# Stick-breaking attention: both heads of a pair in one step, scores on the two row halves in turn, values as float32 products into one bank

## The chip, the cores and the metric

The kernel runs on one core of one Trainium2 chip. The metric is the device time of one execution in microseconds (us); the time of the kernel before is the median of three runs. Engines carry the names of the profile: PE is TensorE (matmuls), PEld its weight loads, DVE VectorE, ACT ScalarE, POOL GpSimd, SP SyncE, whose queue issues the DMAs.

## The reference, cut to what matters

Two layers. Each projects the normalised rows (512 and 16 meta rows, 1,024 wide) into three mixers: stick-breaking attention (6 heads of 64), retention (6 heads of 64) and an S5 state-space mixer (256 wide). Their outputs go through one output projection, and an MLP follows. The part that is changed:

```python
def stick_breaking(q, k, v):
    for blk in range(L // CHUNK):
        z = jnp.einsum('bhqd,bhkd->bhqk', qb, kb).astype(jnp.float32) * scale
        mask = (s_idx[None, :] < t_idx[:, None]) & (s_idx[None, :] >= PAD_FRONT)
        log1m = jnp.where(mask, jax.nn.log_sigmoid(-z), 0.0)
        between = lax.cumsum(log1m, axis=3, reverse=True) - log1m
        w = jnp.where(mask, jnp.exp(jax.nn.log_sigmoid(z) + between), 0.0)
        outs.append(jnp.einsum('bhqk,bhkd->bhqd', w.astype(vb.dtype), vb))
    return jnp.concatenate(outs, axis=2)
```

## The kernel before, in words

Activations lie transposed: 128 channels on the partitions, 528 rows (16 meta rows and 512) along the free axis. A pair of 64-channel heads fills one tile of 128 partitions, so there are three pairs of stick-breaking heads, three pairs of retention heads, and two tiles of S5. Most weights and activations are split into a rounded part (`hi`, `wh`, `xh`) and a rest (`lo`, `wl`, `xl`), and `mm3` makes three products of them for each 128 x 128 block of weights.

**One order for everything, made while the program is built.** `mm3` emits the large projections one matmul after another, and after each step `tick` lets up to `TICKS` waiting tasks go on. A task is a generator (one attention group, one retention pair, the S5 lane, a norm of heads); it emits a few instructions and gives way. It goes on when a modelled clock of the engines (`busy`, fed by `spend`) has reached its time and its condition holds. The engines run what was emitted in that order. Two counters limit the tasks: `free["bank"]`, 5 of the 8 PSUM banks (`BANKS`), from which a task takes banks and to which it gives them back, and `free["group"]` (`GROUPS`, 7), the score groups in flight.

**Score groups.** The lower triangle of a head's 528 x 528 scores is cut into three groups of columns, each in one bank `z`: A (pieces of 272, 144 and 16 columns), B2 (256, 144, 16) and B1 (256, 256). `sb_group` (L815) takes one bank, adds the mask as a bfloat16 product with the identity where the group has one, and adds the score products `z<-sq,sk`, float32, with a contraction of 64: one head lies on one half of the partitions. ACT and DVE then make softplus, POOL and ACT split it, triangular and ones matrices sum it on PE into the same bank (`z<-hi,tri`, `z<-hi,ones`), ACT takes the exponential `e`, and `slow_split` cuts `e` into `hi` (ACT) and `lo` (POOL).

**Values.** `sb_head` (L856) runs one head: group A, then B2 and B1. The values stand as [hi | lo] side by side in 128 columns (`vparts`, L894), and `av` gathers `v x hi` and `v x lo` of `e` over 128 partitions; ACT copies the lower half (`avl`), DVE adds it to the upper half (`sbo`), and when both heads of a pair are done, `slow_split` cuts `sbo` for the output projection (`mix[p]`). Two lanes, `sb_lane(0)` and `sb_lane(1)` (L1083), each go through the three pairs by themselves.

**The rest of a layer.** `ret_lane` runs the three retention pairs (`rtp` transposes, `kv`, `sc`, `ro`, `hps`), `s5_lane` the S5 mixer: a scan, `yps` matmuls, eight `ysm` operations for each of two halves, a gelu on `y`, then `s5_glu` (L789), two `mm3` of `hi`/`lo` of `ysm` with the weights `wglu` (rows `pj<-hi,hi`, `pj<-lo,hi`, `pj<-hi,lo`), a sigmoid and a product. All take banks from the same five. The output projection of a layer comes in three parts: `OUT_PARTS[0]` is (0,1,2), (6,7), (3,4,5), where 0 to 2 are the stick-breaking pairs, 3 to 5 the retention pairs and 6 and 7 S5. Ahead of each part `drain` lets tasks go on, without any projection between them, until the part's inputs have been emitted. In layer 1 the order is (6,7), (0,1,2), (3,4,5).

Nearly all operations of DVE, ACT and POOL carry the line of the helper `issue` (L121), all matmuls but transposes L132, transposes L138.

Of the kernel before, what the change touches and what calls it, by code (L numbers as in the profile page):

```python
# [15 lines left out]
P = 128  # L16
# [5 lines left out]
DFF = 2816  # L22
NF = DFF // P
HALF = T // 2
NT_SLOTS = 60
AHEAD = 4
WLAG = 1000
LEAD = 200
# [1 line left out]
DMA = 3500  # L30
TICKS = 6
BANKS = 5
GROUPS = 7
HOLD = (2, 0)
WENG = (1, 1, 0)
EPS = 1e-6
# [52 lines left out]
def hybrid_kernel(ctx, tc, A, out, dbg=None):  # L89
# [70 lines left out]
    def bank(s="b"):  # L160
        return mx.tile([P, 512], F32, tag="mx", name=nm(s))
# [16 lines left out]
    def banks(n):  # L178
        yield from take("bank", n)
# [676 lines left out]
    def sb_head(q, k, v, hh, o):  # L856

        r = slice(64 * hh, 64 * hh + 64)
        def weights(groups):
            hl, ws = {}, {}  # L860
# [7 lines left out]
        yield from take("group", len(sets[0]))  # L868
        started.append(weights(sets[0]))
        for groups in sets:  # L870
            ws = started[-1]
            if groups is sets[0]:
                yield from take("group", len(sets[1]))
                started.append(weights(sets[1]))
            yield lambda: len(ws) == len(groups)
# [8 lines left out]
            ws.clear()  # L884
            yield
            freed(len(groups), "group")
# [7 lines left out]
    def vparts(vt):  # L894

        v = vp.tile([P, 1280], F32R, tag="v", name=nm("v"))
        v4 = v.rearrange("p (j h c) -> p j h c", h=2, c=P)
        for j0, nj in ((0, 4), (4, 1)):
            yield from banks(1)
            ps = bank("vps")  # L900
            for j in range(nj):
                TE.transpose(ps[:, P * j:P * j + P], vt[:, KT0[j0 + j]:KT0[j0 + j] + P], ident)
            yield
            pv = ps[:, :P * nj].rearrange("p (j h d) -> p j h d", h=2, d=64)
            for hh in range(2):
                SC.copy(out=v4[:, j0:j0 + nj, hh, 0:64], in_=pv[:, :, hh, :])
            yield
            for hh in range(2):
                V.tensor_tensor(out=v4[:, j0:j0 + nj, hh, 64:128], in0=pv[:, :, hh, :],
                                in1=v4[:, j0:j0 + nj, hh, 0:64].bitcast(F32), op=ALU.subtract)  # L910
            yield
            freed(1)
        return v4


    def rotate(t, p, which):
# [137 lines left out]
    for l in range(LAYERS):  # L1054
# [15 lines left out]
        def after(n, p, t, l=l, got=got):  # L1070

            yield
            if n in ("sq", "sk"):
# [2 lines left out]
                yield from headnorm(t, (94 if n == "rq" else 96) + l)  # L1076
                t = yield from rotate(t, p, 0 if n == "rq" else 1)
            elif n == "sv":
                yield lambda: p < 2 or (("done", p - 2, 0) in got and ("done", p - 2, 1) in got)
                t = yield from vparts(t)  # L1080
            got[n, p] = t

        def sb_lane(hh, l=l, got=got, mix=mix):  # L1083
            for p in range(3):
                yield lambda: all((n, p) in got for n in ("sq", "sk", "sv"))
                if ("sbo", p) not in got:
                    got["sbo", p] = tt("sbo")
                yield from sb_head(got["sq", p], got["sk", p], got["sv", p], hh, got["sbo", p])
                got["done", p, hh] = True
                if ("done", p, 1 - hh) in got:  # L1090
                    dump(f"sb{l}{p}", got["sbo", p])
                    mix[p] = yield from slow_split(got["sbo", p])

        def ret_lane(l=l, got=got, mix=mix):
            for p in range(3):
# [12 lines left out]
                mix[6 + i] = yield from slow_split(so[i])  # L1108

        spawn(s5_lane())  # L1110
        spawn(sb_lane(0))
        spawn(sb_lane(1))
        spawn(ret_lane())
        held = []
        for i, (n, p) in enumerate(proj_order(l)):
# [157 lines left out]
```

## Time and profile before

| | us |
|---|---|
| three runs | 1392.8, 1395.85, 1401.91 |
| median | 1395.85 |
| the profiled execution, its own time | 1399.35 |
| its span in the profile | 1397.6 |

The profiled execution is one run apart from the three. Its span is what the rows below add up to, and 1.75 us lie around it. The page of the profile gives busy time by engine, the chain of work that ended last, and groups of instructions by line and shape; the trace adds the timeline of one engine in a stretch, the waits by what ended them, and windows with the clock that TensorE was granted (1.00 is 2.4 GHz, 0.50 is 1.2 GHz). A row of a timeline is a run of equal instructions: its start, its length, and their number; a run's modelled end reaches past the start of the next, so the distance of two starts is what a run costs PE. A float32 product of the score kind leaves two MATMUL records, one of the rounded kind (`hi`, `lo`, `wh`, `wl`) leaves one.

### The profile page before, as it was taken

How to read it: one execution, taken by the hardware profiler on the slowest of the kernel's cores; microseconds unless marked ns; L12 is line 12 of the kernel's file. 1: busy time of each engine (PE TensorE's matmuls, PEld its weight loads, DVE VectorE, ACT ScalarE, POOL GpSimd, SP SyncE). 2: the span in 40 equal slices, each digit the busy share in tenths (PEclk: the TensorE clock that was granted, in tenths of full speed). 3: DMA queues.
4: the chain of work that ended last, by engine and by line, in shares of the span. 5: the costliest groups of instructions: out<-in, count | busy, mean ns of one | idle time of the engine just before them, and what ended most of it. 6: DMA issues, size and time to landing. Idle time of an engine off the chain costs nothing.

```text
span 1397.6 us, 22767 instructions
## 1 busy us (share of the span) xinstructions
PE 1370.0 (98%) x9188; PEld 1254.3 (90%) x9188; DVE 807.1 (58%) x1312; ACT 618.9 (44%) x1002; POOL 509.2 (36%) x624
## 2 busy tenths in 40 slices
PE   6999999999999999999999999999999999999998
PEld 6989898999999999999999999998788888888886
DVE  8875557767455545544566477464585543553453
ACT  5456565545343223322354564874363432442231
POOL 5685536322689302200233544362122210220020
PEclk9999799999999999999999999999999999999999
DMA  4212102313221322222222121122232322223223
GB/s 154 69 65 96 38 21 84 97 46 115 97 76 61 106 91 91 90 93 87 80 91 91 61 93 46 56 68 82 79 106 96 100 92 94 101 91 104 93 77 105
DMA packets 38985, 118.27 MB, mean 85 GB/s; under 512 B 4960, under 2 KB 5472, under 8 KB 38880
## 3 DMA queue, kind: packets, MB, share of 16 engines
q1 hardware_dynamic: 38880, 116.82, 25.8%
q8 instruction: 72, 1.18, 0.3%
q14 instruction: 33, 0.27, 0.1%
HBM read 111.46 MB, written 2.10 MB: 81 GB/s over the span
## 4 chain that ended last, share of the span: by engine, by line
PE 85%; DVE 8%; POOL 4%; issue 1%; DMA 1%; ACT 1%; SPq 0%; DVEq 0%; POOLq 0%; ACTq 0%
PE pj L132 71%; PE z L132 6%; PE hps L132 1%; PE ro L132 1%; PE av L132 1%; DVE s5w L121 1%; PE sc L132 1%; PE yps L132 1%; DVE wl L121 1%; POOL lo L121 1%; PE kps L132 1%; DVE sq L121 1%; DVE gg L121 1%; DVE fr L121 0%; PE kv L132 0%
## 5 line engine op out<-in xcount | busy, mean ns | idle before, releaser
L132 PE MATMUL pj<-xh,wh 128*128 128x264 f32 (+1 forms) x1792 | 451.5, 311 | 13.7 <-ACT wh L121 5.2
L132 PE MATMUL pj<-xh,wl 128*128 128x264 f32 (+1 forms) x1792 | 451.6, 311 | 1.6 <-DVE wl L121 1.6
L132 PE MATMUL pj<-xl,wh 128*128 128x264 f32 (+1 forms) x1792 | 449.7, 310 | 1.7 <-DVE xl L121 1.7
L121 ACT CAST wh<-wr 128x1024 fp32r<-128x1024 f32 (+3 forms) x209 | 206.0, 987 | 417.5 <-PE pj L132 381.8
L132 PEld LDWEIGHTS pj<-xh,wh 128*128 128x128 f32 x1792 | 298.3, 191 | 31.3 <-issue 7.5
L132 PEld LDWEIGHTS pj<-xl,wh 128*128 128x128 f32 x1792 | 298.5, 190 | 19.6 <-DVE xl L121 2.4
L132 PEld LDWEIGHTS pj<-xh,wl 128*128 128x128 f32 x1792 | 298.2, 190 | 19.3 <-issue 2.0
L121 DVE TENSOR_TENSOR wl<-wr,wh 128x1024 fp32r<-128x1024 f32 (+3 forms) x166 | 249.2, 1502 | 73.7 <-ACT wh L121 71.3
L132 PE MATMUL pj<-hi,wh 128*128 128x264 f32 (+1 forms) x720 | 192.9, 323 | 0.0
L132 PE MATMUL pj<-lo,wh 128*128 128x264 f32 (+1 forms) x720 | 192.3, 321 | 0.0
L132 PE MATMUL pj<-hi,wl 128*128 128x264 f32 (+1 forms) x720 | 191.7, 321 | 0.1
L121 POOL TENSOR_TENSOR up<-ga,up 128x528 f32<-128x528 f32 (+1 forms) x44 | 61.8, 1405 | 345.6 <-DVE up L121 345.6
L121 DVE TENSOR_TENSOR h<-h,pj 128x264 f32<-128x264 f32 (+1 forms) x144 | 69.2, 511 | 135.1 <-PE pj L132 135.0
L121 POOL TENSOR_TENSOR wl<-wr,wh 128x1024 fp32r<-128x1024 f32 (+2 forms) x43 | 95.6, 2223 | 130.4 <-ACT wh L121 122.9
L132 PEld LDWEIGHTS pj<-hi,wh 128*128 128x128 f32 x720 | 119.4, 188 | 11.0 <-ACT wh L121 0.6
L132 PEld LDWEIGHTS pj<-hi,wl 128*128 128x128 f32 x720 | 119.4, 188 | 10.9 <-DVE wl L121 0.5
L132 PEld LDWEIGHTS pj<-lo,wh 128*128 128x128 f32 x720 | 119.4, 188 | 10.3
L121 POOL TENSOR_TENSOR lo<-ga,hi 128x528 fp32r<-128x528 f32 (+1 forms) x44 | 58.9, 1339 | 158.7 <-ACT hi L121 158.6
L121 DVE TENSOR_TENSOR up<-pj,R 128x264 f32<-128x264 f32 (+1 forms) x66 | 32.2, 515 | 95.2 <-PE pj L132 95.2
L121 ACT ACTIVATE si<-si,bias 128x528 f32<-128x528 f32 (+1 forms) x44 | 32.1, 731 | 94.3 <-DVE si L121 94.3
L121 DVE TENSOR_TENSOR ga<-si,up 128x528 f32<-128x528 f32 (+1 forms) x44 | 31.7, 720 | 72.7 <-ACT si L121 56.8
L121 ACT ACTIVATE e<-z 128x512 f32<-128x512 f32 (+2 forms) x72 | 39.3, 546 | 63.2 <-PE z L132 57.2
(228 smaller groups left out, 1747.1 us busy)
## 6 DMA issues: line engine op xcount, KB each, us to landing
wr<-in_w_in_dram SPq DMA_DIRECT2D x45, 512.0 KB, 3.5
wr<-in_w_gate_dram SPq DMA_DIRECT2D x44, 512.0 KB, 3.4
wr<-in_w_up_dram SPq DMA_DIRECT2D x44, 512.0 KB, 3.4
wr<-in_w_down_dram SPq DMA_DIRECT2D x32, 512.0 KB, 3.4
wr<-in_w_out_dram SPq DMA_DIRECT2D x16, 384.0 KB, 3.2
wr<-in_w_down_dram SPq DMA_DIRECT2D x16, 384.0 KB, 3.1
rc<-in_rope_dram SPq DMA_DIRECT2D x12, 264.0 KB, 3.7
rs<-in_rope_dram SPq DMA_DIRECT2D x12, 264.0 KB, 4.0
```

The lines of the kernel that those rows point to most:

```text
L121: return f(*a, **k)
L132: nc.tensor.matmul(out, lhsT=lhsT, rhs=rhs, start=start, stop=stop, skip_group_check=more)
```

## The change

One lane now runs both heads of a pair. `sb_scores` takes two banks and emits the products of the two heads in turn: head 0 on the partitions 0 to 63, head 1 on 64 to 127, each into its own bank. The scores' chain on the other engines (`sb_group`) stays as it was, up to `e`. `e` is no longer split: the values stand as float32 (`by_keys`), and `av` gathers both heads in one bank, head 0 on the output partitions 0 to 63 and head 1 on 64 to 127, with float32 products. `avl`, `sbo` and their split give way to one `hi` and one `lo` from `av` itself. Three lanes are started, one for each pair, and the next pair begins when the one before has all its weights `e`. `GROUPS` goes from 7 to 8, the tile slots from 60 to 62, and `mm`'s modelled cost of a product on half of the rows or columns is halved. `BANKS` stays at 5 and `OUT_PARTS` as it is.

```diff
-NT_SLOTS = 60
+NT_SLOTS = 62
-GROUPS = 7
+GROUPS = 8
...
-        spend("PE", 2 * max(107.0, 2 * n) if rhs.dtype == F32 else max(107.0, n) + 3)
+        t = 2 * max(107.0, 2 * n) if rhs.dtype == F32 else max(107.0, n) + 3
+        spend("PE", t / 2 if 64 in (rhs.shape[0], out.shape[0]) else t)
...
-    def sb_group(q, k, r, g, gi, place, hl, ws):
-
+    def sb_scores(q, k, g):
 
         n = width(g)
-        yield from banks(1)
-        zp = bank("z")
         m = masks.get(n)
+        zs = [bank("z"), bank("z")]
         if m is not None:
-            mm(zp[:, :n], lhsT=identb, rhs=m, start=True, stop=False)
+            for z in zs:
+                mm(z[:, :n], lhsT=identb, rhs=m, start=True, stop=False)
         for j, q0, q1, o0 in g:
-            mm(zp[:, o0:o0 + q1 - q0], lhsT=k[r, KT0[j]:KT0[j] + P], rhs=q[r, q0:q1],
-               start=m is None and j == g[0][0], stop=j == g[-1][0], more=m is None)
+            for hh, z in enumerate(zs):
+                r = slice(64 * hh, 64 * hh + 64)
+                mm(z[:, o0:o0 + q1 - q0], lhsT=k[r, KT0[j]:KT0[j] + P], rhs=q[r, q0:q1],
+                   start=m is None and j == g[0][0], stop=j == g[-1][0], more=m is None)
+        return zs
...
-        ws[gi] = yield from slow_split(e, n, G)
+        ws[gi] = e
...
+            def one(gi, g):
+                yield from banks(2)
+                zs = sb_scores(q, k, g)
+                for hh in range(2):
+                    spawn(sb_group(zs[hh], g, gi, place, hl[hh], ws[hh]), now[0][1])
             for gi, g in enumerate(groups):
-                spawn(sb_group(q, k, r, g, gi, place, hl, ws), now[0][1])
+                spawn(one(gi, g), now[0][1])
...
-                for part in range(2):
-                    mm(av[:, q0 - qa:q1 - qa], lhsT=v[:, j, hh, :], rhs=ws[gi][part][:, o0:o0 + q1 - q0],
-                       start=n == 0 and part == 0, stop=n == len(todo) - 1 and part == 1)
...
+                for hh in range(2):
+                    mm(av[64 * hh:64 * hh + 64, q0 - qa:q1 - qa], lhsT=v[:, P * j + 64 * hh:P * j + 64 * hh + 64],
+                       rhs=ws[hh][gi][:, o0:o0 + q1 - q0], start=n == 0, stop=n == len(todo) - 1)
...
-            lo = tt("avl")
-            SC.copy(out=lo[0:64, :qb - qa], in_=av[64:128, :qb - qa])
-            yield
-            V.tensor_tensor(out=o[r, qa:qb], in0=lo[0:64, :qb - qa], in1=av[0:64, :qb - qa], op=ALU.add)
+            if hi is None:
+                hi, lo = tt("hi"), tt("lo")
+            SC.copy(out=R_(hi[:, qa:qb]), in_=av[:, :qb - qa])
+            yield
+            V.tensor_tensor(out=R_(lo[:, qa:qb]), in0=av[:, :qb - qa], in1=hi[:, qa:qb], op=ALU.subtract)
...
-        def sb_lane(hh, l=l, got=got, mix=mix):
-            for p in range(3):
-                yield lambda: all((n, p) in got for n in ("sq", "sk", "sv"))
...
+        def sb_lane(p, l=l, got=got, mix=mix):
+            yield lambda: all((n, p) in got for n in ("sq", "sk", "sv")) and (p == 0 or ("sb", p - 1) in got)
+            res = []
+            yield from sb_pair(got["sq", p], got["sk", p], got["sv", p], lambda: got.update({("sb", p): True}), res)
+            mix[p] = res[0]
```

The order of the instructions moves with it. On PE, at the first score groups of layer 0, the program before has one head's group A and then that head's B2 (`z_1050`, `z_1055` are banks, `sq_491` the queries and `sk_494` the keys of pair 0):

```order
L132 LDWEIGHTS identb
L132 MATMUL z_1050<-maskA,identb 128x432
L132 MATMUL z_1050<-sq_491,sk_494 128x272
L132 MATMUL z_1050<-sq_491,sk_494 128x144
L132 MATMUL z_1050<-sq_491,sk_494 128x16
L132 LDWEIGHTS identb
L132 MATMUL z_1055<-maskB_99,identb 128x416
L132 MATMUL z_1055<-sq_491,sk_494 128x256
L132 MATMUL z_1055<-sq_491,sk_494 128x144
L132 MATMUL z_1055<-sq_491,sk_494 128x16
```

At the same place of PE the changed program has group A of both heads (`z_899`, `z_900`):

```order
L133 LDWEIGHTS identb
L133 MATMUL z_899<-maskA,identb 128x432
L133 LDWEIGHTS identb
L133 MATMUL z_900<-maskA,identb 128x432
L133 MATMUL z_899<-sq_491,sk_494 128x272
L133 MATMUL z_900<-sq_491,sk_494 128x272
L133 MATMUL z_899<-sq_491,sk_494 128x144
L133 MATMUL z_900<-sq_491,sk_494 128x144
L133 MATMUL z_899<-sq_491,sk_494 128x16
L133 MATMUL z_900<-sq_491,sk_494 128x16
```

The masks now come two in a row, and each piece of one head is followed by the same piece of the other. On PE again, in layer 0, the program before has this behind the last `yps` of S5 (`rtp_3016` is a transpose of a retention pair's values, `av_3023` the values of a stick-breaking head); further `av`, `kv` and `sc` matmuls and the rest of the layer's projections follow:

```order
L132 MATMUL yps_3009<-xi_2807,gg_647 128x131
L138 MATMUL rtp_3016<-ident,rv_2668 16x128
L132 MATMUL av_3023<-hi_2962,v_1890 128x256
L132 MATMUL av_3023<-lo_2963,v_1890 128x256
L132 MATMUL av_3023<-hi_2962,v_1890 128x256
L132 MATMUL av_3023<-lo_2963,v_1890 128x256
```

In the changed program the last `yps` of layer 0 is followed by eight `pj` of the output part (0,1,2), whose last is the first row here, and then by one retention pair alone (`rm`, `rv` its rotated and transposed tiles); behind its 14 `ro` come the two `hps`, the 24 products of `s5_glu`, and the second output part (6,7):

```order
L133 MATMUL pj_3208<-hi_2460,wl_3073 128x264
L139 MATMUL rtp_3252<-ident,rv_2325 16x128
L133 MATMUL kv_3263<-rv_3213,kt_3214 128x128 x4
L133 MATMUL sc_3285<-rm_2227,rm_2606 128x128 x4
L133 MATMUL sc_3286<-rm_2227,rm_2606 16x16
L133 MATMUL sc_3296<-rm_2227,rm_2606 128x128 x4
L133 MATMUL sc_3297<-rm_2227,rm_2606 16x16
L133 MATMUL ro_3311<-sc_3284,rv_3213 64x128
```

The last `yps` has moved from ahead of projections and attention to the end of the first output part. The `av` of the pairs are all ahead of it now. On ACT the same stretch of the changed program, the S5 tail of layer 0 (`ysm` and `y` are S5's, `o`, `ro` and `hsq` the retention pair's):

```order
L121 CAST hi_3321<-ysm_2390 128x528
L121 ACTIVATE y_478_3268<-y_478_3268 128x528
L121 ACTIVATE y_478_3268<-y_478_3268,bias 128x528
L121 COPY o_3330<-ro_3311 128x512
L121 ACTIVATE y_478_3268<-y_478_3268 128x528
L121 COPY o_3330<-ro_3312 128x16
L121 CAST hi_3334<-ysm_3123 128x528
L121 ACTIVATE hsq_3337<-o_3330 128x528
```

The copy of `ro` stands ahead of the third pass of `y` here; in the program before the two copies of `ro` stand there likewise, ahead of the third pass.

## Rows read from the trace of the kernel before

**Rows 1.** The page, busy time of each engine, its share of the span, instructions.

```profile
PE 1370.0 (98%) x9188; PEld 1254.3 (90%) x9188; DVE 807.1 (58%) x1312; ACT 618.9 (44%) x1002; POOL 509.2 (36%) x624
```

**Rows 2.** The page, the chain that ended last, share of the span by engine.

```profile
PE 85%; DVE 8%; POOL 4%; issue 1%; DMA 1%; ACT 1%; SPq 0%; DVEq 0%; POOLq 0%; ACTq 0%
```

**Rows 3.** Waits of PE: for what; total us, times, longest.

```profile
PE z L132 <- POOL lo L121: 1.2, 2, 0.6
```

**Rows 4.** Timeline of PE, one head's A and B groups: start, length, instruction, records.

```profile
139.34 0.36 PE L132 MATMUL z<-maskA,identb 128*128 128x432 bf16 x1
139.62 1.09 PE L132 MATMUL z<-sq,sk 64*128 64x272 f32 x6
140.65 0.35 PE L132 MATMUL z<-maskB,identb 128*128 128x416 bf16 x1
140.93 2.03 PE L132 MATMUL z<-sq,sk 64*128 64x256 f32 x10
142.89 0.51 PE L132 MATMUL pj<-xh,wl 128*128 128x264 f32 x2
```

**Rows 5.** Timeline of PE, a B2 group and a B1 group alone.

```profile
80.89 1.07 PE L132 MATMUL z<-sq,sk 64*128 64x256 f32 x6
81.89 0.52 PE L132 MATMUL pj<-xh,wh 128*128 128x264 f32 x2
...
108.47 1.13 PE L132 MATMUL z<-sq,sk 64*128 64x256 f32 x4
109.52 0.51 PE L132 MATMUL pj<-xh,wl 128*128 128x264 f32 x2
```

**Rows 6.** Timeline of PE, values of one head: first set, then second set.

```profile
114.64 0.28 PE L132 MATMUL av<-hi,v 128*128 128x272 f32 x1
...
115.25 0.49 PE L132 MATMUL pj<-xl,wh 128*128 128x264 f32 x2
115.58 0.40 PE L132 MATMUL pj<-xh,wl 128*128 128x264 f32 x2
115.82 0.40 PE L132 MATMUL pj<-xh,wh 128*128 128x264 f32 x2
...
226.08 0.28 PE L132 MATMUL av<-hi,v 128*128 128x256 f32 x1
...
227.14 0.49 PE L132 MATMUL pj<-xh,wl 128*128 128x264 f32 x2
```

**Rows 7.** Timeline of PE, retention: products on column halves, and on row halves.

```profile
196.02 0.44 PE L132 MATMUL ro<-sc,rv 128*64 128x128 f32 x4
196.39 0.49 PE L132 MATMUL ro<-rm,st 128*128 128x128 f32 x2
196.80 0.44 PE L132 MATMUL ro<-sc,rv 128*64 128x128 f32 x4
...
260.05 1.30 PE L132 MATMUL sc<-rm,rm 64*128 64x128 f32 x10
261.27 0.39 PE L132 MATMUL pj<-xl,wh 128*128 128x264 f32 x1
```

**Rows 8.** Timelines of PE and DVE, the S5 tail of layer 0.

```profile
252.38 0.39 PE L132 MATMUL yps<-xi,gg 128*128 128x131 f32 x2
...
274.65 0.60 PE L132 MATMUL pj<-hi,hi 128*128 128x264 f32 x2
...
287.43 1.32 DVE L121 TENSOR_TENSOR lo<-glu,hi 128x528 fp32r<-128x528 f32 x2
```

**Rows 9.** Groups by shape: count, busy us, mean ns, idle before.

```profile
L121 DVE SCALAR_TENSOR_TENSOR ysm<-u,cols,yps 32x132 f32<-32x132 f32 x64 | 28.9, 451 | 9.3 <-PE yps L132 8.4
...
L121 POOL TENSOR_TENSOR lo<-e,hi 128x512 fp32r<-128x512 f32 x12 | 16.5, 1374 | 13.1 <-ACT hi L121 13.1
...
L121 ACT ACTIVATE y<-y 128x528 f32<-128x528 f32 x8 | 5.2, 645 | 3.1 <-DVE y L121 3.1
...
L121 ACT COPY o<-ro 128x512 f32<-128x512 f32 x6 | 3.5, 586 | 13.8 <-PE ro L132 13.8
```

**Rows 10.** Windows: length, busy of PE, PEld, DVE, ACT, POOL, PE clock, DMA.

```profile
158.60:175.70 17.10, 17.10 (x70) 15.24 (x69) 3.54 (x10) 8.89 (x20) 6.84 (x7) 0.50 0.10 31
383.90:390.70 6.80, 5.42 (x24) 5.45 (x25) 4.77 (x8) 2.03 (x3) 6.73 (x12) 0.50 0.22 75
```

More of the change, by code (lines that the diff above doesn't have):

```diff
@@ L812, in s5_glu, with sb_group @@
             yield
[L815 removed]
+    def sb_scores(q, k, g):
         n = width(g)
[L819 to L820 removed]
         m = masks.get(n)
+        zs = [bank("z"), bank("z")]
         if m is not None:
[L823 removed]
+            for z in zs:
+                mm(z[:, :n], lhsT=identb, rhs=m, start=True, stop=False)
         for j, q0, q1, o0 in g:
[L825 to L826 removed]
+            for hh, z in enumerate(zs):
[3 more added lines that the diff above has]
+        return zs
+    def sb_group(zp, g, gi, place, hl, ws):
+        n = width(g)
         yield
@@ L853, in sb_group, with sb_pair @@
         freed(1)
-        ws[gi] = yield from slow_split(e, n, G)
-    def sb_head(q, k, v, hh, o):
-        r = slice(64 * hh, 64 * hh + 64)
+        ws[gi] = e
+    def sb_pair(q, k, v, go, res):
         def weights(groups):
-            hl, ws = {}, {}
+            hl, ws = ({}, {}), ({}, {})
             place = {j: (gi, o0, q0) for gi, g in enumerate(groups) for j, q0, q1, o0 in g}
+            def one(gi, g):
[3 more added lines that the diff above has]
+                    spawn(sb_group(zs[hh], g, gi, place, hl[hh], ws[hh]), now[0][1])
             for gi, g in enumerate(groups):
-                spawn(sb_group(q, k, r, g, gi, place, hl, ws), now[0][1])
+                spawn(one(gi, g), now[0][1])
             return ws
@@ L867, in sb_head @@
         sets = ((G_A,), (G_B2, G_B1))
-        yield from take("group", len(sets[0]))
+        yield from take("group", 2)
         started.append(weights(sets[0]))
+        hi = lo = None
         for groups in sets:
@@ L872, in sb_head @@
             if groups is sets[0]:
-                yield from take("group", len(sets[1]))
+                yield from take("group", 4)
                 started.append(weights(sets[1]))
-            yield lambda: len(ws) == len(groups)
+            yield lambda: all(len(w) == len(groups) for w in ws)
+            if groups is sets[1]:
+                go()
             yield from banks(1)
@@ L880, in sb_head, with by_keys @@
             for n, (gi, (j, q0, q1, o0)) in enumerate(todo):
-                for part in range(2):
-                    mm(av[:, q0 - qa:q1 - qa], lhsT=v[:, j, hh, :], rhs=ws[gi][part][:, o0:o0 + q1 - q0],
-                       start=n == 0 and part == 0, stop=n == len(todo) - 1 and part == 1)
-            ws.clear()
+                for hh in range(2):
+                    mm(av[64 * hh:64 * hh + 64, q0 - qa:q1 - qa], lhsT=v[:, P * j + 64 * hh:P * j + 64 * hh + 64],
+                       rhs=ws[hh][gi][:, o0:o0 + q1 - q0], start=n == 0, stop=n == len(todo) - 1)
+            for w in ws:
+                w.clear()
             yield
-            freed(len(groups), "group")
-            lo = tt("avl")
-            SC.copy(out=lo[0:64, :qb - qa], in_=av[64:128, :qb - qa])
+            freed(2 * len(groups), "group")
+            if hi is None:
+                hi, lo = tt("hi"), tt("lo")
+            SC.copy(out=R_(hi[:, qa:qb]), in_=av[:, :qb - qa])
             yield
-            V.tensor_tensor(out=o[r, qa:qb], in0=lo[0:64, :qb - qa], in1=av[0:64, :qb - qa], op=ALU.add)
+            V.tensor_tensor(out=R_(lo[:, qa:qb]), in0=av[:, :qb - qa], in1=hi[:, qa:qb], op=ALU.subtract)
             yield
             freed(1)
-    def vparts(vt):
-        v = vp.tile([P, 1280], F32R, tag="v", name=nm("v"))
-        v4 = v.rearrange("p (j h c) -> p j h c", h=2, c=P)
+        res.append((R_(hi), R_(lo)))
+    def by_keys(vt):
+        v = vp.tile([P, 640], F32, tag="v", name=nm("v"))
         for j0, nj in ((0, 4), (4, 1)):
@@ L903, in vparts @@
             yield
-            pv = ps[:, :P * nj].rearrange("p (j h d) -> p j h d", h=2, d=64)
-            for hh in range(2):
-                SC.copy(out=v4[:, j0:j0 + nj, hh, 0:64], in_=pv[:, :, hh, :])
-            yield
-            for hh in range(2):
-                V.tensor_tensor(out=v4[:, j0:j0 + nj, hh, 64:128], in0=pv[:, :, hh, :],
-                                in1=v4[:, j0:j0 + nj, hh, 0:64].bitcast(F32), op=ALU.subtract)
+            SC.copy(out=v[:, P * j0:P * (j0 + nj)], in_=ps[:, :P * nj])
             yield
             freed(1)
-        return v4
+        return v
     def rotate(t, p, which):
@@ L1068, in scaled, with after @@
             return t
-        def after(n, p, t, l=l, got=got):
+        def after(n, p, t, l=l, got=got, mix=mix):
             yield
@@ L1078, in after @@
             elif n == "sv":
-                yield lambda: p < 2 or (("done", p - 2, 0) in got and ("done", p - 2, 1) in got)
-                t = yield from vparts(t)
+                yield lambda: p < 2 or mix[p - 2] is not None
+                t = yield from by_keys(t)
             got[n, p] = t
-        def sb_lane(hh, l=l, got=got, mix=mix):
-            for p in range(3):
-                yield lambda: all((n, p) in got for n in ("sq", "sk", "sv"))
[L1086 to L1092, printed above, removed]
+        def sb_lane(p, l=l, got=got, mix=mix):
[3 more added lines that the diff above has]
+            mix[p] = res[0]
         def ret_lane(l=l, got=got, mix=mix):
@@ L1110, in hybrid_kernel @@
         spawn(s5_lane())
-        spawn(sb_lane(0))
-        spawn(sb_lane(1))
+        for p in range(3):
+            spawn(sb_lane(p))
         spawn(ret_lane())
```

## The prediction, made before the changed kernel ran

> **What bounds the kernel now.** I read the page first: PE is busy for 1370.0 of 1397.6 us [rows 1], and the chain that ended last lies on PE for 85% [rows 2]. The list of waits has few entries for PE, and of those that the change touches only one, the scores' bank waiting for POOL's rest of the split, twice, 1.2 us in all [rows 3]. So two questions decide: how much PE time the change takes out, and whether the new order leaves PE without work anywhere. DVE, ACT and POOL are busy for 58, 44 and 36% [rows 1]; what is taken from them counts only where PE waits. PE's timeline then gives the price of the score and value runs, as the distance of two starts, and the windows show where PE's clock was granted at 0.50.
>
> **Scores.** One head's group A costs 139.62 to 140.65, 1.03 us, for 432 columns as float32; B2 and B1 in a row 1.96 us [rows 4]; alone they cost 1.00 and 1.06 [rows 5]. Twelve heads (six in each layer) at 1.03 + 1.96 are 35.9 us. If the two row halves work at the same time, a pair costs as much as a head alone: six pairs at 1.03 + 1.00 + 1.06 are 18.5 us. That removes 17.4. The two masks now come one behind the other, so the second one is spared the change of mode: a mask of 432 columns takes 0.28 [rows 4], at the pace of 264 columns in 0.12 us [rows 6] it would be 0.20; about 0.1 for twelve groups, 1.2 less. Against it, the pieces of 16 columns hardly stream at all, and four weight loads follow one another for each pair of them: an estimated 0.1 for 12 such pairs, 1.2 more. **Scores: -17.4.** The trace of before has no run in which the two row halves alternate, so this is bounded: if they don't overlap at all, only changes of mode are saved, those at the masks, 1.2, and one entry for two heads in each of 18 group pairs at an estimated 0.12, 2.1, together 3.3. I take the full overlap because the column halves show it: two products of 128 columns on two column halves cost 0.37 us (196.02 to 196.39), while five row-half products one after another cost 1.22, 0.24 each with the small one among them [rows 7].
>
> The Trainium skill says the same of row tiles, in "TensorE: Matmul & The Clock Gate", the part on packing small matmuls, with a loss: four row tiles measured 3.07 times the speed of one, not four. An estimate from that figure (77% of the ideal) would leave about 4 us less of the gain; no run here shows it for two halves.
>
> **Values.** The first set of a head costs 0.61 us, the second 1.06 [rows 6]; 12 x 1.67 = 20.0 us. Afterwards each product is float32, four passes of the columns where `hi` and `lo` were two, but on both column halves at once: 1,360 columns x 4 passes at 0.12 us for 264 are 2.47 us per pair, 14.8 for six. Entering and leaving the column mode costs 0.14 a run (the 0.37 of [rows 7] less the 0.23 that 128 columns x 4 passes take at that pace); the order has 17 such runs, 2.4 us, and the 16-column pieces add an estimated 1.8. That is 19.0. **Values: -1.0**, between 0 and -3.
>
> **The split of e.** POOL's `lo<-e` (36 of them, a 512-column one takes 1.37 us [rows 9]) and ACT's `hi<-e` go, and so do `avl`, `sbo` and the split of the values. They lie beside PE's work, so I give them only the 1.2 us of waits [rows 3]. **-1.2.** `by_keys` and the new `hi`/`lo` of `av` are fewer operations than what they replace, hidden in the same cover. The counters and slots cost no time by themselves.
>
> **What the new order does to S5 in layer 0.** This is the step against the change. A group of a pair holds two banks at once, and the next pair starts when the one before has its weights; attention therefore holds four of the five task banks for most of the projections, and the S5 lane and the retention pairs, which take from the same five, come later. In layer 0 the last `yps` now stands at the end of the first output part, and behind it there is no projection left to fill PE (the order shows it behind `pj_3208`). What is left for PE before the part (6,7) is: 8 `pj` (1.0 us), the transposes, `kv`, ten `sc` (1.3) and 14 `ro` (3.1 by [rows 7]) of one retention pair, two `hps`, 24 products of `s5_glu` (2.9) and the transposes of the next pair: 12.9 us in all. Meanwhile S5 has to go through its tail. Bare, from the last `yps`: 8 `ysm` at 0.45 are 3.6; the gelu on ACT and DVE, 8 operations on 528 columns at 0.65, two of them shorter, 4.8; `hi` and `lo`, 1.3; the 24 products, 2.9; clamp, three ACT passes, product, `hi` and `lo` of the second tile, 4.4, with 1.7 of the first tile's passes ahead of them on ACT: 18.7 us (0.45 and 0.65 from [rows 9], 0.66 for a `lo` from [rows 8]). But the order puts the retention pair's work among them: its copy of `ro` stands ahead of the last pass of `y` on ACT, so that `y` waits until PE has done `ro`, some 3.5 us, and ten ACT operations of that pair (copies, its norm, the gate) cost about 6.3 at 0.59 to 0.65 [rows 9]. That makes 28.5. PE then waits 28.5 - 12.9 = **15.6 us**. Bounds: the bare chain gives 18.7 - 12.9 = 5.8; the time that this tail took in the trace of before, from the `yps` run at 252.38 to the end of `lo<-glu` at 288.75, 36.3 us [rows 8], gives 23.4. In before PE had projections and output products all the while, so it cost nothing. I take 15.6 because it counts what the order has there, and it lies in the middle.
>
> The last retention pair of layer 0 comes in the third part with a cover of about 4.4 us of output products for a chain of 6 to 7: **+2**. Behind a wait of that length the clock can fall: at 383.9 to 390.7 in the trace of before it stood at 0.50 behind a pause of PE, and 5.42 us of PE work [rows 10] took twice as long as at 1.00: **+2.7**. The other such stretch lasted 17.1 us and cost half of it, 8.5 [rows 10]; it may come again or not, in either kernel. In layer 1 the S5 part stands first and S5 is early in both orders, nothing is added there.
>
> The Trainium skill has a rule on this, "TensorEngine Tiling (Array Packing)", Gotcha 1: PSUM Pressure: different row tiles need different banks, so packing rows raises the demand for them. The row for it here is the order, where a pair's group takes two banks; the trace of before can't show a wait for banks, since the waits are settled while the program is built.
>
> **The sum.** On the profiled execution: 1399.35 - 17.4 - 1.0 - 1.2 + 15.6 + 2 + 2.7 = 1400.1. That execution lies 3.5 above the median of the three runs, so against the median the forecast is 1396.5, I say 1396: the gain on PE is given back in S5's tail. Its own range is 1388 (the longer half-clock stretch doesn't come again) to 1403.
>
> **Rivals.**
> Rival 1, the wait at S5's tail is short: the engines run ahead of the order where they can, and PE waits only for the bare chain, 5.8, with no fall of the clock. That is 12.5 less: 1384, and 1375.5 if the longer half-clock stretch goes as well. For it speaks that DVE, ACT and POOL have less work in attention than before, against it that ACT takes its operations in order.
> Rival 2, on the slower side: the row halves don't work side by side. The scores then save 3.3 and not 17.4, and the same waits come to 1399.35 - 3.3 - 1.0 - 1.2 + 20.3 = 1414.2, less 3.5: 1410.7. It decides as soon as a pair's group costs more than 1.8 us instead of 1.03. For it: no row shows the overlap for row halves; against it: [rows 7] for column halves.
> Rival 3: the tail takes as long as in before (23.4 us of wait), and the clock stays at 0.50 as long as in the longer stretch (8.5 instead of 2.7): 1413.7, less 3.5 is 1410. Against it: DVE and ACT have fewer other tasks in that stretch than before.
>
> **How the numbers follow.** The forecast has 0.55, rival 1 0.25, rival 2 0.12, rival 3 0.08. A difference under 1%, 14 us, can't be told from none in this kernel. Faster by over 1% (under 1381.9): half of rival 1 and a little of the forecast, 0.18. Slower by over 1% (over 1409.8): half or more of rivals 2 and 3 and the tail of the forecast, 0.16. Within 1%: 0.66. The range goes from rival 1's low end, 1375, to rivals 2 and 3, 1412.
>
> **What the profile after would show.** Score runs of a pair of about 1.0 to 1.1 us for A, with alternating records that start almost together; if 1.9, rival 2. Runs of `av` of 2.5 to 3.2 us per pair. In layer 0, PE idle ahead of the products of the part (6,7), put down to DVE's `lo<-glu`, for about 15 us; 6 or less would be rival 1, 23 rival 3. A wait ahead of the third part of about 2. A half-clock stretch behind the wait. What would make the prediction wrong altogether: that the longer delays of S5 and retention reach the first output part as well, or that ACT or DVE, not PE, hold the projections of layer 0.

## The result, and the profile after

The changed kernel takes 1407.18 us (median of 8 runs, 1404.68 to 1409.45), the kernel before 1395.7 in the same measurement (8 runs, 1388.93 to 1401.91): ratio 1.0085, interval 1.0063 to 1.0106. It is slower by 0.85%, inside the 1% that I called no change and inside the range (1375 to 1412), 11 us above the predicted 1396. But the interval leaves out 1: the forecast was no change, and the kernel did get slower. With eight runs on each side a difference well under the 14 us of the prediction can be told. The profiled execution took 1406.12, its span is 1404.4.

The page, busy time by engine and the chain that ended last, answering to [rows 1, 2]:

```profile
PE 1358.3 (97%) x9188; PEld 1235.4 (88%) x9188; DVE 793.6 (57%) x1270; ACT 589.1 (42%) x936; POOL 467.4 (33%) x588
...
PE 71%; POOL 3%; DVE 3%; issue 1%; ACT 1%; DMA 0%; DVEq 0%
```

(The shares of the chain after add up to 79% only, so its 71% is not to be compared with the 85% of before.) PE is busy for 11.7 us less, and yet the span is 6.8 longer: what PE saved went into waiting, and more. The list of PE's waits (what for; total us, times, longest) has entries that the kernel before hadn't, or had smaller:

```profile
PE pj L133 <- ACT hi L121: 7.1, 1, 7.1
PE wps L139 <- POOL py L121: 5.8, 1, 5.8
...
PE pj L133 <- DVE lo L121: 3.3, 1, 3.3
PE hps L133 <- ACT hsq L121: 2.9, 2, 2.3
PE ro L133 <- DVE sc L121: 2.8, 2, 1.5
```

The 7.1, the 2.8 and 2.3 of the 2.9 lie in S5's tail in layer 0. The wait for POOL's `lo` ahead of `z` [rows 3] is gone, as forecast. The scores of the first pair on PE's timeline, against [rows 4, 5]:

```profile
67.64 0.54 PE L133 MATMUL z<-maskA,identb 128*128 128x432 bf16 x2
68.11 1.10 PE L133 MATMUL z<-sq,sk 64*128 64x272 f32 x12
69.14 0.53 PE L133 MATMUL z<-maskB,identb 128*128 128x416 bf16 x2
69.60 1.07 PE L133 MATMUL z<-sq,sk 64*128 64x256 f32 x12
```

Group A of two heads, 12 records, costs 1.03 us (68.11 to 69.14), what six records of one head cost before. On PE's timeline, the values of a pair's first set in layer 1, and of a second one (in two pieces):

```profile
934.70 1.00 PE L133 MATMUL av<-e,v 128*64 128x272 f32 x12
935.63 0.51 PE L133 MATMUL pj<-xh,wh 128*128 128x264 f32 x2
...
953.85 0.65 PE L133 MATMUL av<-e,v 128*64 128x256 f32 x2
954.43 0.66 PE L139 MATMUL rtp<-ident,rm 128*128 128x128 f32 x4
...
956.99 1.83 PE L133 MATMUL av<-e,v 128*64 128x256 f32 x18
958.75 0.51 PE L133 MATMUL pj<-xl,wh 128*128 128x264 f32 x2
```

0.93 + 0.58 + 1.76 = 3.27 us a pair, 19.6 for six, against 20.0 [rows 6] and my 19.0. That is one pair, and a little over the 2.5 to 3.2 that I had named. Added up over all runs in the two traces (distances of starts, those at 0.50 halved), the scores went from 36.4 to 19.4 us, the masks from 6.7 to 5.5, and the values from 21.2 to 19.0. S5's tail in layer 0 on PE, from the last `yps` on (in brackets the wait ahead of the run and what ended it):

```profile
272.36 0.39 PE L133 MATMUL yps<-xi,gg 128*128 128x131 f32 x2
...
278.90 0.85 PE L133 MATMUL ro<-sc,rv 128*64 128x128 f32 x4 [1.30 <-DVE sc L121]
281.21 1.12 PE L133 MATMUL ro<-sc,rv 128*64 128x128 f32 x6 [1.46 <-DVE sc L121]
...
288.93 2.13 PE L133 MATMUL hps<-hsq,blk 128*128 128x264 f32 x4 [2.31 <-ACT hsq L121]
290.48 1.01 PE L133 MATMUL pj<-hi,hi 128*128 128x264 f32 x2
...
303.26 0.81 PE L133 MATMUL pj<-hi,wh 128*128 128x264 f32 x2 [7.07 <-ACT hi L121]
```

The part (6,7) begins at 303.26, 30.9 us behind the start of the last `yps`; PE waits 12.1 of them (12.3 with a pause of 0.14 in a row that isn't shown). The last wait ended with ACT's `hi<-glu`, and not with DVE's `lo<-glu` as I had named; 5.1 of the rest lie ahead of the retention pair's `ro` and `hps`. ACT's timeline shows why the tail is long: the copy of `ro` runs between two passes of `y`, and the gate's passes (`sg`) run between those of `glu`, as the order had it.

```profile
282.77 0.74 ACT L121 ACTIVATE y<-y,bias 128x528 f32<-128x528 f32 x1
285.80 0.59 ACT L121 COPY o<-ro 128x512 f32<-128x512 f32 x1 [2.29 <-PE ro L133]
286.28 0.65 ACT L121 ACTIVATE y<-y 128x528 f32<-128x528 f32 x1
...
298.82 0.62 ACT L121 ACTIVATE sg<-sg 128x528 f32<-128x528 f32 x1
299.36 0.72 ACT L121 ACTIVATE glu<-glu,bias 128x528 f32<-128x528 f32 x1
299.98 1.16 ACT L121 ACTIVATE glu<-glu 128x528 f32<-128x528 f32 x2
302.05 0.63 ACT L121 CAST hi<-o 128x528 fp32r<-128x528 f32 x1 [0.91 <-DVE o L121]
302.58 1.16 ACT L121 CAST hi<-glu 128x528 fp32r<-128x528 f32 x2
```

The windows in which PE's clock was granted at 0.50 (columns as in [rows 10]):

```profile
27.46:34.28 6.82, 5.79 (x26) 5.80 (x27) 6.56 (x33) 1.68 (x2) 1.88 (x4) 0.50 0.44 154
85.48:92.31 6.83, 6.00 (x26) 5.96 (x27) 4.40 (x9) 3.42 (x6) 6.76 (x13) 0.50 0.20 67
187.88:191.30 3.42, 3.42 (x18) 3.42 (x18) 3.42 (x4) 1.09 (x2) 3.11 (x3) 0.50 0.08 20
280.04:293.70 13.66, 10.18 (x41) 7.95 (x42) 5.19 (x12) 5.35 (x10) 1.73 (x4) 0.50 0.03 10
300.52:307.35 6.83, 4.07 (x17) 3.76 (x18) 3.94 (x6) 2.80 (x6) 0.79 (x2) 0.50 0.00 0
396.10:399.51 3.41, 3.41 (x18) 3.41 (x17) 1.88 (x2) 1.38 (x2) 3.33 (x6) 0.50 0.38 125
802.28:809.11 6.83, 6.83 (x34) 5.28 (x31) 1.15 (x2) 4.31 (x10) 0.00 (x0) 0.50 0.27 93
...
sum 47.80, PE 39.70 PEld 35.58 DVE 26.53 ACT 20.02 POOL 17.60; mean PE 5.67 PEld 5.08 DVE 3.79 ACT 2.86 POOL 2.51
```

These give a measure that I use below: PE's busy time less half of what it did at 0.50, **PE's work at the full clock**. After: 1358.3 - 39.7/2 = 1338.5. Before, with 25.9 us of PE work in three such stretches (those of [rows 10] and this one), 1370.0 - 13.0 = 1357.0:

```profile
18.67:22.08 3.41, 3.41 (x16) 3.41 (x17) 3.41 (x9) 1.10 (x2) 2.92 (x2) 0.50 0.01 2
```

So the change took 18.5 us of work from PE, and gave 18.5 us of waits (27.6 to 46.1 us of the span without PE busy) and 6.9 us of half clock (39.7 less 25.9, halved) in return: +6.9.

### The profile page after: what moved, and what is told of

It reads as the page before. It is cut to its first block, busy times and chain, and to the rows that moved or that the text cites. A ratio compares the mean times of both kernels' runs of the same rounds, so it can differ in the third digit from the quotient of the medians.

```text
span 1404.4 us, 22537 instructions
## 1 busy us (share of the span) xinstructions
PE 1358.3 (97%) x9188; PEld 1235.4 (88%) x9188; DVE 793.6 (57%) x1270; ACT 589.1 (42%) x936; POOL 467.4 (33%) x588
## 4 chain that ended last, share of the span: by engine, by line
PE 71%; POOL 3%; DVE 3%; issue 1%; ACT 1%; DMA 0%; DVEq 0%
PE pj L133 64%; PE z L133 3%; PE hps L133 1%; PE ro L133 1%; PE av L133 1%; POOL st L121 1%; PE sc L133 1%; DVE ysm L121 1%; DVE wl L121 0%; POOL gx L121 0%; POOL lo L121 0%; POOL py L121 0%; POOL bb L121 0%; PE kv L133 0%; PE yps L133 0%
## 5 line engine op out<-in xcount | busy, mean ns | idle before, releaser
L133 PEld LDWEIGHTS pj<-hi,wh 128*128 128x128 f32 x720 | 120.6, 189 | 19.6 <-ACT hi L121 7.4
L121 POOL TENSOR_TENSOR lo<-sp,hi 128x432 fp32r<-128x432 f32 (+2 forms) x36 | 47.2, 1329 | 26.4 <-ACT hi L121 26.2
```

What stands on the lines that cost most here:

```text
L121: return f(*a, **k)
```

## The experiments

All are compared with runs of the kernel before on the same chip; these medians lay between 1396.2 and 1397.4 for e1 to e11. "Tail wait" is what PE waits between layer 0's last `yps` and the end of `lo<-glu`, pauses over 0.1 us. PE's work is read from one profiled execution each. In the eight kernels with the changed kernel's scores, side by side, and its values (changed, e3 to e5, e7 to e9, e11) it lies between 1337.1 and 1340.4, so a difference under about 3 us says little.

| kernel | median us | ratio, interval | PE's work at full clock | tail wait |
|---|---|---|---|---|
| before | 1395.7 | | 1357.0 | 0 |
| changed | 1407.18 | 1.0085, 1.0063 to 1.0106 | 1338.5 | 12.3 |
| e1 scores in order | 1411.61 | 1.0104, 1.0079 to 1.013 | 1343.5 | 12.3 |
| e2 old values | 1398.91 | 1.003, 1.0013 to 1.0047 | 1340.8 | 5.0 |
| e3 full model cost | 1381.57 | 0.9896, 0.9874 to 0.9918 | 1339.1 | 0 |
| e4 one bank left | 1394.15 | 0.9977, 0.9966 to 0.9988 | 1339.9 | 5.1 |
| e5 by two | 1404.44 (one run) | | 1337.5 | 12.0 |
| e6 before, half cost | 1395.74 | 0.999, 0.9977 to 1.0003 | 1355.9 | 1.1 |
| e7 full cost, bank left | 1380.78 | 0.9893, 0.9859 to 0.9927 | 1338.6 | 0 |
| e8 full cost, B late | 1391.87 | 0.9949, 0.9921 to 0.9978 | 1340.4 | 1.4 |
| e9 full cost, phasors later | 1373.27 | 0.9831, 0.9809 to 0.9854 | 1337.1 | 0.3 |
| e10 before, phasors later | 1400.83 | 1.0039, 1.0018 to 1.006 | 1356.5 | 1.8 |
| e11 changed, phasors later | 1381.08 | 0.9882, 0.9864 to 0.99 | 1337.2 | 4.2 |

**My theory:** the scores side by side take some 17 us from PE, the values 1; it is given back in S5's tail, which the pairs' banks make late. **Rivals:** the scores' gain has another source than the alternation; the halved modelled cost, not the banks, makes S5 late.

### e1: the scores head by head

```diff
-        for j, q0, q1, o0 in g:
-            for hh, z in enumerate(zs):
-                r = slice(64 * hh, 64 * hh + 64)
+        for hh, z in enumerate(zs):
+            r = slice(64 * hh, 64 * hh + 64)
+            for j, q0, q1, o0 in g:
```

> The changed kernel, but in sb_scores all products of head 0 are emitted ahead of those of head 1; all other work and its order stay. If the gain of the scores comes from the two row halves running side by side when they alternate: a pair's group A goes from 1.03 us to about 1.9 to 2.06, PE's busy time rises by 13 to 15 us over the changed kernel's 1358.3, and the time is about 1420 (1407 + 14). If it comes from the two heads being in one step (fewer changes of mode, masks together), or PE itself looks past the products of one half: under 3 us more, 1407 to 1410.

Neither. PE's busy time rose by 8.0 us, PE's work by 5.0 and the median by 4.4; the intervals of the two ratios overlap, so the rows decide. PE's timeline of e1:

```profile
68.73 1.66 PE L133 MATMUL z<-sq,sk 64*128 64x272 f32 x12
70.33 0.53 PE L133 MATMUL z<-maskB,identb 128*128 128x416 bf16 x2
70.78 1.61 PE L133 MATMUL z<-sq,sk 64*128 64x256 f32 x12
72.32 0.52 PE L133 MATMUL pj<-xh,wh 128*128 128x264 f32 x2
```

Group A of the pair costs 1.60, not 1.03 and not 2.06, and B2 1.54, not 1.00 and not 2.00. The starts of records of A in the trace, in us (the trace gives the columns of a record; the head is inferred from them and from the order within a head):

```
69.065  272 columns, head 0, second record
69.295  144 columns, head 0, first record
69.300  272 columns, head 1, first record
69.417  144 columns, head 0, second record
69.540   16 columns, head 0, first record
```

Head 1's first product starts beside head 0's second one, ahead of records that were emitted before it; four records of head 0 were then left, with the one that had just started. In the emitted order all six records of head 0 come first, so the columns alone show that PE departs from it. And group B1, which has four records a head, keeps its full overlap in e1: the two heads start 13 ns apart. So the gain comes from the two row halves at once, but without the alternation PE still takes nearly half of it in A and B2 and all of it in B1, by starting work on the other half early.

### e5: blocks of two products

```diff
-        for j, q0, q1, o0 in g:
-            for hh, z in enumerate(zs):
-                r = slice(64 * hh, 64 * hh + 64)
+        for hh, js in ((0, g[:2]), (1, g[:2]), (0, g[2:]), (1, g[2:])):
+            z, r = zs[hh], slice(64 * hh, 64 * hh + 64)
+            for j, q0, q1, o0 in js:
```

> The changed kernel with the score products in blocks: two products of head 0 (272 and 144 columns), two of head 1, then the 16-column one of each; groups of two products are emitted head by head. With head by head in order, the run of a pair's A group cost 1.60 us against 1.03 when alternating, and head 1's first product began only when four records of head 0 were left, while B1 (two products, four records a head) still began its two heads 13 ns apart. If PE starts the other row half's product as soon as no more than four records stand ahead of it, A and B2 cost 1.03 and 1.00 again, and PE's busy time at full clock is 1338 to 1340. If what counts is strict alternation, A costs 1.3 to 1.6.

With four records of one head ahead of the other's, hardly anything is lost: 1.04 for A (68.61 to 69.65), 1.01 for B2, and 1337.5 of work at the full clock, just under the 1338 that I expected. On PE's timeline of e5:

```profile
68.61 1.11 PE L133 MATMUL z<-sq,sk 64*128 64x272 f32 x12
69.65 0.53 PE L133 MATMUL z<-maskB,identb 128*128 128x416 bf16 x2
```

### e2: the values as before

```diff
-        ws[gi] = e
+        ws[gi] = yield from slow_split(e, n, G)
...
-            for n, (gi, (j, q0, q1, o0)) in enumerate(todo):
-                for hh in range(2):
-                    mm(av[64 * hh:64 * hh + 64, q0 - qa:q1 - qa], lhsT=v[:, P * j + 64 * hh:P * j + 64 * hh + 64],
-                       rhs=ws[hh][gi][:, o0:o0 + q1 - q0], start=n == 0, stop=n == len(todo) - 1)
+            for hh in range(2):
+                if hh:
+                    yield from banks(1)
+                av = bank("av")
+                for n, (gi, (j, q0, q1, o0)) in enumerate(todo):
+                    for part in range(2):
+                        mm(av[:, q0 - qa:q1 - qa], lhsT=v[:, j, hh, :], rhs=ws[hh][gi][part][:, o0:o0 + q1 - q0],
+                           start=n == 0 and part == 0, stop=n == len(todo) - 1 and part == 1)
...
```

> The changed kernel with the values as before: e split into hi and lo, values as hi and lo side by side in 128 columns, av per head, avl, sbo and its split; the scores stay alternating on the row halves. (60 tile slots instead of 62.) If the float32 values on column halves are worth the 1.0 us of my sum: PE's busy time, counted at the full clock, rises by 0 to 3, and the 36 lo<-e on POOL come back without cost beyond 1 to 2 us of waits, time 1405 to 1412. If the split of e on POOL and ACT held PE more than that, it shows as waits of PE for POOL lo or ACT hi of 4 us or more.

PE's work is 2.3 higher than in the changed kernel, within the 0 to 3 expected but also within what the order alone moves. The median is 8 us lower, below the range. The trace shows only a part of that, since the profiled execution, 1404.63, is the slowest of the ten and lies 1.5 us under the changed kernel's. In it the last `yps` comes as late as in the changed kernel (272.1), but 98 products of the output part follow it and not eight, so the tail waits 5.0 and not 12.3 us, and a new wait of 5.5 stands ahead of an `av`. What made the other nine runs faster wasn't seen; their granted clock is 0.985 to 0.989, the profiled one's 0.985. So the values part by itself isn't shown to be worth more than a few us in either direction.

### e3, e4, e7: what makes S5 late

e3 undoes one line, the modelled cost; e4 leaves one bank; e7 does both.

```diff
-        spend("PE", t / 2 if 64 in (rhs.shape[0], out.shape[0]) else t)
+        spend("PE", t)
```

```diff
             def one(gi, g):
+                yield lambda: free["bank"] >= 3
                 yield from banks(2)
```

> The changed kernel with one line undone: mm counts a product on half of the rows or columns at its full modelled cost, as before. Nothing that is computed changes, only the order; the pairs still hold two banks each. My prediction held that the banks of the pairs make S5 late in layer 0. If so, the S5 tail stays late and PE waits 10 to 15 us ahead of the part (6,7), time 1400 to 1410. Rival: the halved modelled cost makes it late. Then the last yps of layer 0 comes well ahead of the end of the projections, the waits of 12.1 us between 277 and 303 us and the half-clock stretches at 280 and 300 us (5.1 + 2.0 us) go, and the time is 1384 to 1392.

> The changed kernel, but a pair's group takes its two banks only when three are free, so that one task bank is left to S5 and retention; the modelled cost stays halved. By my theory of the banks S5's last yps of layer 0 comes about 200 rows of PE's order earlier, the wait ahead of the part (6,7) falls from 7.1 to under 3 us, and the time is 1388 to 1397; attention itself ends later, which may cost a wait of some us ahead of the part (0,1,2). By the rival (the modelled cost alone) nothing moves by more than 4 us: 1403 to 1410.

> The two edits together: full modelled cost, and a pair's group takes two banks only when three are free. If each frees S5 and nothing else, both together give no more than the full cost alone, 1379 to 1384. If the pairs' banks still cost something in the full-cost order (retention, norms waiting for a bank), it is faster by 3 to 6: 1376 to 1379. If attention now ends late and the part (0,1,2) waits for it, 1384 to 1392.

e3 came out on the rival's side, and below its range: last `yps` at 221.9 instead of 272.5 us, no wait in the tail, 1381.57, faster than before by 1.04%. Between the two profiled executions lie 23.4 us: 11.4 of waits and 12.7 of half clock, less 0.6 of work. The tail accounts for 19.4 of it (12.3 of waits, 7.1 of half clock); elsewhere half clock falls by 5.6 more, and other waits grow by 0.9. e4 came out on mine: with the modelled cost still halved the last `yps` comes at 247.7, the 7.1 us wait is gone, and the predicted price appears, attention ends late: 1394.15. PE waits 4.5 us for it at 256 us, which with 0.6 more is all of the 5.1 in the table. The last `yps` (the second record of each run), first in e3, then in e4:

```profile
221.77 0.39 PE L133 MATMUL yps<-xi,gg 128*128 128x131 f32 x2
...
247.63 0.39 PE L133 MATMUL yps<-xi,gg 128*128 128x131 f32 x2
```

So in this order the halved cost needs the pairs' hold on the banks to make S5 late, and either edit removes the wait. e7 (1380.78, as expected if each frees S5 and nothing else) adds nothing to e3 that the intervals could tell. PE's longest waits in e3:

```profile
PE wps L139 <- DVE u L121: 7.0, 1, 7.0
PE pj L133 <- ACT wh L121: 5.3, 1, 5.3
PE pj L133 <- DVE ga L121: 3.6, 1, 3.6
```

The second and third are as in the kernel before (5.2 and 3.6); the first is the wait at 80 us, which the tail's fix leaves standing.

### e6: the halved modelled cost in the kernel before

```diff
-        spend("PE", 2 * max(107.0, 2 * n) if rhs.dtype == F32 else max(107.0, n) + 3)
+        t = 2 * max(107.0, 2 * n) if rhs.dtype == F32 else max(107.0, n) + 3
+        spend("PE", t / 2 if 64 in (rhs.shape[0], out.shape[0]) else t)
```

> The kernel before with nothing but the halved modelled cost of products on half of the rows or columns. Nothing that is computed changes. If the halved cost by itself makes S5 late in layer 0, PE waits there by 5 us or more in this kernel too, and the time is 1400 to 1410. If it takes the pairs' two banks as well (both together), S5 stays under cover (the order has its last yps some 35 rows later only) and the time stays at 1391 to 1400.

No change, 0.999: S5's tail waits 1.1 us. In the kernel before, where each group takes one bank, the halved cost does no harm.

### e8: S5 late, at the full cost

```diff
             if groups is sets[0]:
+                yield lambda: bool(ready)
                 yield from take("group", 4)
```

(`ready` is the list of S5's parameters.)

> Full modelled cost, and the second set (B2, B1) of each pair starts only when the S5 parameters have been made, which in layer 0 leaves the banks to the parameters' transposes at 80 us and moves attention, and with it S5's last yps, some 210 rows of PE's order back, into the first output part. If a late S5 tail is what costs time, whatever made it late, the wait of 7 us at 80 us goes and one of 6 to 13 us comes ahead of the part (6,7), with a half-clock stretch: 1383 to 1394, slower than the full cost alone (1381.6). If the full cost helped in some other way (attention's pace), the time falls by the 7 us of the early wait and its half-clock stretch: 1371 to 1376.

A miss on both sides. The last `yps` comes at 258.7, 37 us later than in e3, and still PE waits only 1.4 us in the tail: some 130 products of the output parts stand behind it, where the changed kernel had eight. Late was no loss where there was cover. The wait at 78 us did not go either (5.7 us, now for DVE's `u` ahead of `hps`), which spoke against my reading of it as a wait for a bank. The median, 1391.87, is 10 above e3 all the same, inside the first range but not for its reason: its ten runs spread from 1381.1 at a mean granted clock of 0.995 to 1395.55 at 0.984; the profiled one is among the quick ones (1381.16). What lowers the clock in the others wasn't seen.

### e9, e10, e11: the early wait

```diff
             n = 1
+            if l == 0:
+                yield lambda: len(over) >= 3
             while n < NCH:
                 yield
```

`over` lists the finished parts of S5's parameters. The chain of small `py` and `st` operations of S5's phasors, on DVE and POOL, starts later in layer 0: in e9 at the full cost, in e10 in the kernel before, in e11 in the changed kernel.

> The full-cost kernel, and in layer 0 the chain of small S5 parameter operations (py, st on DVE and POOL) starts only when the S5 input and output matrices are made. In the changed kernel and in the full-cost one PE waits 5.8 and 7.0 us at 80 us for a DVE whose queue is full of that chain, and a half-clock stretch follows (3.0 and 2.0 us). If that chain is the cause, the wait falls under 2 us and the time to 1370 to 1377, unless S5, which needs the chain's results, becomes late (its last yps stands 127 rows of PE's order later, still ahead of the output parts): then a wait of 3 us or more comes in its tail. If the wait is one for a bank held by a score group, it stays, 1379 to 1384.

> The kernel before with the chain of small S5 parameter operations started only when the matrices are made. In its trace PE waits 0.5 and 2.0 us at 70 to 75 us for that chain, and its long half-clock stretch at 158 us stands behind another wait. If the gain of this edit depends on the early score groups of the pairs, it is small here: 1390 to 1397. If the edit is worth the same in any order (7 to 9 us), 1387 to 1390.

> The changed kernel, with its halved modelled cost, and only the chain of small S5 parameter operations started later. By the order, S5's last yps in layer 0 then stands at the start of the output parts, not at the end of the first. If a tail without cover is what costs, whatever made it late, both the early wait (5.8 us) and most of the tail's 12.3 us and their half-clock stretches go: 1373 to 1383. If the halved cost is bad by itself, the tail's wait stays: 1394 to 1400.

e9 is the fastest, 1373.27, 1.7% under the kernel before and in the expected range. Its longest waits of PE:

```profile
PE pj L133 <- ACT wh L121: 5.3, 1, 5.3
PE pj L133 <- DVE ga L121: 3.8, 1, 3.8
PE pj L133 <- DVE wl L121: 3.2, 1, 3.2
PE yps L133 <- DVE rq L121: 3.1, 1, 3.1
```

The 7.0 at 80 us and the half-clock stretch behind it are gone: the chain, which filled DVE from 70 to 86 us with PE's next bank behind it, was the cause. In e3 the chain's last operation ends at 86.1, and PE waits for `u` behind it (PE's row, then DVE's):

```profile
87.07 1.09 PE L139 MATMUL wps<-ident,ws 128*128 128x128 f32 x4 [6.97 <-DVE u L121]
...
86.50 0.76 DVE L121 TENSOR_TENSOR u<-pj,R 128x264 f32<-128x264 f32 x2
```

Of the 5.9 us between the profiled executions of e3 and e9 only 1.8 are waits, since 1.7 at 67 us and 3.1 at 172 us are new; 2.1 are half clock and 2.0 PE's work. In the kernel before the same edit costs 0.4%, outside the range that I expected: its early waits were small, and S5's last `yps` moves from 252.5 to 270.6 us. e11 (1381.08, within 1373 to 1383) gains 26 us on the changed kernel: 5.8 from the early wait, 8.1 from the tail (12.3 to 4.2: its order has the last `yps` at the start of the output parts), 8.0 from the half clock (PE did 23.7 us at 0.50 instead of 39.7), the rest from smaller waits (2.4) and PE's work (1.3). It keeps the halved modelled cost, so that cost is not bad by itself.

## Why the prediction was right, step by step

**Scores, -17.4 and values, -1.0:** 18.5 us of work went from PE, 18.4 were forecast. That it fits to 0.1 is luck: by their own rows the scores and their masks gave 18.2 and the values 2.2, while PE's other work took 1.9 more, and the order alone moves PE's work by up to 3. The overlap of row halves, for which I had only column halves as evidence, is complete: 1.03 us for one head or two. The estimate of a loss from the 3.07 of the Trainium skill's page "TensorE: Matmul & The Clock Gate" (packing small matmuls), 4 us, found nothing in this case: two float32 products on row halves cost what one costs. Rival 2 is ruled out, and e1 shows that even without alternation PE overlaps a part of it.

**The wait at S5's tail, 15.6:** it is there, at the place named, with the reason named (bare tail behind eight `pj`, the copy of `ro` ahead of `y` on ACT): 12.3. The tail took 32.2 us instead of 28.5 up to the end of `lo<-glu`, but PE went on at 30.9. PE's work in it took 18.8 instead of 12.9, since the half clock (280.04 to 293.70) added 5.1; that hid a part of the wait. e3, e7 and e9 take the wait away, in e3 with 19.4 us between the two traces, so the tail's price is shown; the 25 to 34 us that the three win on the changed kernel are more than the tail. Rival 1 (5.8) and rival 3 (23.4) are both off.

**Why S5 was late:** "attention therefore holds four of the five task banks" was not enough as a cause. The halved modelled cost of the same change had to come with it: without it S5 is early although the pairs hold their banks (e3), and by itself it does nothing to the kernel before (e6). The position of the phasors' chain can undo both (e11). Which task gets the next free bank is a race, and small changes to its clock decide it. The step of my reasoning that S5 is late because of the pairs alone does not hold. That cost the forecast nothing, since the sum took the place of the last `yps` from the order and not from this reason. The other parts of the change that feed the race, three lanes in turn and `GROUPS` at 8, were not tried by themselves.

**The clock, +2.7:** it was 6.9. I had counted one fall, behind a wait; the trace has the seven stretches shown above. Five of them begin inside one of PE's five longest pauses between products (3.3 to 7.1 us) or up to 1.6 us behind its end, three of these ahead of the tail.

**Missed:** the waits at 80 us (5.8) and 184 us (3.3), 4.6 more than before had between 60 and 200 us, and 1.2 more at the start. I looked for waits only where the order left PE without products, not where something else stood in DVE's queue ahead of what PE needs. At 80 us that was the phasors' chain. At 184 us PE waits for the new `lo<-av`, which stands in DVE's queue behind an operation that waits for a DMA of the retention keys:

```profile
184.50 0.71 DVE L121 TENSOR_TENSOR rsw<-rsw,rs 128x528 f32<-128x528 f32 x1 [2.63 <-DMA rsw<-rk]
```

**The last retention pair, +2:** no such wait; its pair found cover in the output part (6,7).

**The sum:** PE's work came to -18.5 for -18.4, the waits to +18.5 in all for 16.4 (-1.2 + 15.6 + 2), the half clock to +6.9 for 2.7. These differences, 6.2, bring the 1400.1 of the sum to the 1406.1 of the profiled execution within 0.2. That the waits fit to 2 us is luck too: the tail and the last pair cost 5.3 less than forecast, and the waits elsewhere 7.4 more. The medians lie 11.5 apart and not 6.8, since the profiled execution of before took 3.6 more than its median and that of after 1.1 less. Whether the half-clock stretch of 17.1 us makes that 3.6 isn't shown, as no other run of the kernel before has a trace.

## What to carry to other kernels

In these runs two float32 products of contraction 64 on different row halves cost PE as much as one, and they need not alternate strictly: two products of one half could stand ahead of the other's (e5), three could not (e1). Where an order is made by tasks that race for banks under a modelled clock, price a change twice: what it takes from the engine, and where the new order leaves a serial tail without cover; here a gain of 18 us turned into a loss of 11, and three small edits to the race (e3, e4, e11) each brought back 13 to 26. Look at the cover behind the last step that a dependent stage waits for, and not at how late it is.

## What the runs showed of the hardware

In these runs PE started a product on one row half ahead of earlier emitted products for the other half as soon as four of their records were left, the running one included (e1: 5 ns behind the third of six records of head 0; e5 and group B1 in e1, with four records: 13 to 14 ns behind the first). Side by side, two heads' records start 6 to 7 ns apart when they alternate. In the tail the clock fell late: the first 4.3 of the 7.1 us of the wait from 296.19 to 303.26 us lie at 1.00, and the half-clock stretch begins at 300.52 and outlasts the wait to 307.35.
